# A two-layer diffusion backbone step: later stores, a lead on each load's space, and another table of slots for seven products

## The chip, the core and the metric

The kernel runs on one core of one Trainium2 chip. A core has TensorE (PE, matmuls into eight PSUM banks), VectorE (DVE), ScalarE (ACT), GpSimd (POOL), a queue of transfers issued by SyncE (SP), and sixteen DMA engines. Each engine works off its own instructions in order; they meet through semaphores. The metric is device time of one execution: 3125.22 us is the median of three runs of the kernel before (3124.19 to 3126.09).

## The reference

One inference step over nine row tiles of 128 tokens (T = 0 is the prompt, T = 1 to 8 the sample) with 1024 channels, in float32. Layer 0 mixes tokens with a gated long convolution (Hyena), layer 1 with differential attention, and each is followed by a gated ConvFFN. What the change touches is the ConvFFN:

```python
def conv_ffn(h, w_up, w_dw, b_dw, w_down):      # h (L, 1024), w_up (1024, 5632), w_down (2816, 1024)
    u = dwconv3(h @ w_up, w_dw, b_dw)           # three taps over the tokens
    g, val = jnp.split(u, 2, axis=-1)
    return (jax.nn.silu(g) * val) @ w_down
# around it: hp = rmsnorm(x)*(1+scale)+shift;  x = x + gate * rmsnorm(conv_ffn(hp))
```

The rest (adaLN rows from `SiLU(cond)`, RMSNorms, the Hyena filter and convolution, q/k/v, softmax differences, output projections) is computed as well and is not changed in what it does.

## The kernel before

**Precision.** A float32 product is made of three float32r products: `hi` is a rounded copy (ACT), `lo` the rest (DVE subtracts, or ACT writes `-hi` and a POOL transfer adds the source to it), and PE does hi·hi, hi·lo, lo·hi. `split` (L213) and `halves` (L222) do this; their lines L215, L217, L218 and L220 stand for all splits.

**Column thirds.** Tokens are cut in three groups c = 0, 1, 2 of three tiles, 386 or 388 columns. In `ffn` (L643), for each of 22 blocks j (or g) of 128 channels of the hidden layer, group 0 is done straight: `up` (L659) of the gate and the value weights (24 matmuls each, L667 to L669), `conv`, `gate_val`, and `down0` (18 matmuls into six pinned banks, L690). This is the *up loop*, g = 0 to 21. Groups 1 and 2 are done together: seven products of half-size blocks in the place of eight (a Strassen-like scheme), 12 matmuls each (L746), in the *stage of seven products*: 22 · 7 = 154 slots t, where slot t runs `product(j, q)` with j, q = divmod(t, 7), and then `along(t)`, the other engines' share. The hidden rows go to DRAM (`hid_d`), and the *down stage* reads them back and multiplies by `ffn_down` (L690).

**The table.** `ALONG` (L800) lists for each q what `along` does: `(d, fn, ...)` means fn for block j + d. `load_pair` issues the two weight loads of a block (512 KB each), `total` makes the sums s1 to s4 (DVE, L719), `both` splits with a POOL transfer, `high` (ACT, L729) and `low` (DVE, L732) split without one, `evac` empties banks, `middle`, `side`, `silu`, `finish` do the three-tap filter, the gate and the store. `along` starts at t = -19 (L817), in the last rounds of the up loop: two values of t after each of three places of a round.

**Queues.** SP issues nearly all loads and stores, in program order: one that waits holds up all behind it. Where a load writes into space of an older buffer, it waits until the older one's last reader is done. `postnorm` (L593) is a generator that `advance` steps; `tail(0)` at t = 1 hands three of them to a queue, one step for each block of the seven products, and `tail(1)` does so in the down stage. `extra0` and `extra1` add adaLN rows: loads `adaw`, two DVE passes each (L379).

**Space.** The program is first recorded without a chip (`Dry`). `take` notes for each buffer its size and the count of instructions when it is taken; `note` when it is last used; a last use that is a transfer gets 40 more instructions (`lag`). `place` (L88) then gives addresses, largest buffers first, with as many spare instructions after a buffer's end as fit (up to 1000), trying the whole lag first, then less of it.

Of the kernel before, what the change touches and what calls it, by code (L numbers as in the profile page):

```python
# [15 lines left out]
P = 128  # L16
D = 1024
KT = 8
# [20 lines left out]
class Dry:  # L39
# [14 lines left out]
    def note(self, *args, **kw):  # L54
        for x in (*args, *kw.values()):
            i = self.of.get(x.tensor.name) if isinstance(x, bass.AP) else None
            if i is not None:
                self.lives[i][2:] = self.clock, self.lag
        self.clock += 1

    def transfer(self, *args, **kw):
# [9 lines left out]
    def take(self, shape, dtype, name):  # L71
        t = self.array(shape, dtype)
        size = 4 * math.prod(shape[1:])
        self.of[t.tensor.name] = len(self.lives)
        self.lives.append([-(-size // 32) * 32, self.clock, self.clock, 0])
        return t

    @contextmanager
# [8 lines left out]

def place(lives, room):  # L88

    size, first, until, lag = np.array(lives, dtype=np.int64).T  # L90
    n, end = len(lives), int((until + lag).max()) + 2
    todo = np.lexsort((first, -size))

    def attempt(fill, last):
# [24 lines left out]
        return at.tolist()  # L119

    for part in (4, 3, 2, 1, 0):
        for percent in range(100, 70, -2):
            at = attempt(percent / 100, until + lag * part // 4)
            if at is not None:
                return at
    raise MemoryError("the buffers do not fit")
# [31 lines left out]
def tile_step(tc, nc, a: dict, cst, mem, banks):  # L158
# [38 lines left out]
    def f(ap):  # L197
        return ap.bitcast(F32)
# [392 lines left out]
    def postnorm(T, x, acc, gs, out=None):  # L591
# [49 lines left out]
    SEVEN = ((0, 0), (4, 1), (5, 2), (3, 3), (1, 0), (6, 2), (2, 3))  # L641
    GROUPS = (3, 2, 2, 2, 2, 2, 2, 2, 2, 3)

    def ffn(l, hs, gs, nxt, queue, extra=iter(()), late=(), after=None):

        raw, spl, hid, accs = {}, {}, {}, {}
        ops, rows, sums, out = {}, {}, {}, {}
        hid_d = [tc.dram_tile((P, 6 * P), F32, name=f"hid{l}_{j}") for j in range(NJ)]

        def load(g, parts=range(3)):  # L650
# [51 lines left out]
                    g == 0, g == NJ - 1)  # L702


        def load_pair(j):
            if j < NJ:
                raw[j] = [bt([KT, P], "wr") for _ in range(2)]
                for i in range(2):
                    sync.dma_start(raw[j][i], a["ffn_up"][l, j, :, i])

        lo, hi = slice(0, 4), slice(4, 8)

        def total(i, j):

            a1, a2 = raw[j]
            x, y, op = ((a2[:, lo], a2[:, hi], ALU.add), (sums.get((1, j)), a1[:, lo], ALU.subtract),
                        (a1[:, lo], a2[:, lo], ALU.subtract), (a1[:, hi], sums.get((2, j)), ALU.subtract))[i - 1]
            t = sums[i, j] = bt([4, P], f"s{i}")
            dve.tensor_tensor(out=t, in0=x, in1=y, op=op)  # L719

        def weight(q, j):

            if q in (1, 2, 3, 6):
                return sums[{1: 2, 2: 3, 3: 1, 6: 4}[q], j]
            return raw[j][q == 5][:, lo if q == 0 else hi]

        def high(q, j):
            ops[j, q] = bt([4, P], "hi", F32R), bt([4, P], "lo", F32R)
            act.activation(ops[j, q][0], weight(q, j), AF.Copy)  # L729

        def low(q, j):
            dve.tensor_tensor(out=ops[j, q][1], in0=weight(q, j), in1=f(ops[j, q][0]), op=ALU.subtract)  # L732

        def both(q, j):
            ops[j, q] = halves(weight(q, j), bt, [4, P], True)

        def product(j, q):
            b, d = SEVEN[q]
            if q < 4:
                out[j, d] = ps("pp", True)  # L740
            pt = out[j, d]
            wh, wl = ops.pop((j, q))
            bh, bl = hs["pair"][b]
            for k in range(4):
                for i, (w, t) in enumerate(((wh, bh), (wh, bl), (wl, bh))):
                    pe.matmul(pt[:, 0:NP], w[:, k, :], t[:, k, :], start=q < 4 and k == 0 and i == 0,  # L746
                              stop=k == 3 and i == 2, skip_group_check=q > 3)

        def add(dst, x, pt):
            dve.tensor_tensor(out=dst, in0=pt, in1=x, op=ALU.add)  # L750

        def evac(q, j):
            if q == 0:
                u = sums["u", j] = st([NP], "u")
                act.activation(u, out[j, 0][:, 0:NP], AF.Copy)  # L755
                rows[j] = [st([2 * NP - 2], "row") for _ in range(2)]
            elif q == 1:
                pt, u = out.pop((j, 1)), sums["u", j]
                add(u, u, pt[:, 0:NP])
                unpin(pt)  # L760
            elif q == 2:
                v = sums["v", j] = st([NP], "v")
                add(v, sums["u", j], out[j, 2][:, 0:NP])
            elif q == 3:
                add(rows[j][1][:, NP - 1:], sums.pop(("v", j))[:, 1:], out[j, 3][:, 1:NP])
            elif q == 4:
                pt = out.pop((j, 0))
                act.activation(rows[j][0][:, 0:NP - 1], pt[:, 0:NP - 1], AF.Copy)
                unpin(pt)
            elif q == 5:  # L770
                pt = out.pop((j, 2))
                add(rows[j][1][:, 0:NP - 1], sums["u", j][:, 0:NP - 1], pt[:, 0:NP - 1])
                unpin(pt)
            else:
                pt = out.pop((j, 3))
                add(rows[j][0][:, NP - 1:], sums.pop(("u", j))[:, 1:], pt[:, 1:NP])
                unpin(pt)
# [14 lines left out]
        def side(i, e, j):  # L792
# [4 lines left out]
                rows[j][i] = rows.pop((j, i))  # L797


        ALONG = (  # L800
            ((-1, middle, 1), (0, total, 4), (-2, finish), (-1, evac, 6)),
            ((-1, side, 1, 0), (-1, side, 1, 1), (1, both, 0), (0, high, 6), (0, evac, 0)),
            ((3, load_pair), (-1, middle, 0), (2, total, 1), (0, low, 6), (0, evac, 1)),
            ((1, both, 2), (-1, side, 0, 0), (2, total, 2), (0, evac, 2)),
            ((2, high, 1), (1, both, 3), (-1, side, 0, 1), (0, evac, 3)),
            ((2, low, 1), (1, both, 5), (0, evac, 4)),
            ((-1, silu), (1, both, 4), (2, total, 3), (0, evac, 5)))

        def along(t):
            j, q = divmod(t, 7)  # L810
            for d, fn, *args in ALONG[q]:
                if 0 <= j + d < NJ:
                    fn(*args, j + d)

        def along2(ts):
            for t in (next(ts), next(ts)):
                if t >= -19:  # L817
                    along(t)


# [50 lines left out]
        def main():  # L871
# [25 lines left out]
            advance(queue, -1)  # L897
            for t in range(7 * NJ):
                j, q = divmod(t, 7)
                product(j, q)  # L900
                along(t)
                if t == 1:
                    down0(NJ - 1)
# [13 lines left out]
            for i, (c, m) in enumerate(groups):  # L917
# [1452 lines left out]
```

## Time and profile before

| | |
|---|---|
| median of three runs | 3125.22 us |
| the profiled execution | 3126.71 us, its span 3124.9 us |
| granted clock, mean over the span | 0.992 |
| PE busy, of the span | 97% |
| DVE, ACT, POOL busy | 69%, 55%, 20% |
| DMA queues of SP and of POOL, share of 16 engines | 37.9%, 19.5% |

Matmuls are pipelined: a 386-column one is busy for 0.34 us and the next starts 0.18 us after it, so busy PE is no measure of what could be saved; idle stretches and stretches at the lower clock are.

### The profile page before, as it was taken

How to read it: one execution, taken by the hardware profiler on the slowest of the kernel's cores; microseconds unless marked ns; L12 is line 12 of the kernel's file. 1: busy time of each engine (PE TensorE's matmuls, PEld its weight loads, DVE VectorE, ACT ScalarE, POOL GpSimd, SP SyncE). 2: the span in 40 equal slices, each digit the busy share in tenths (PEclk: the TensorE clock that was granted, in tenths of full speed). 3: DMA queues.
4: the chain of work that ended last, by engine and by line, in shares of the span. 5: the costliest groups of instructions: out<-in, count | busy, mean ns of one | idle time of the engine just before them, and what ended most of it. 6: DMA issues, size and time to landing. Idle time of an engine off the chain costs nothing. (4 is left out here: it accounts for less than half of the span.)

```text
span 3124.9 us, 46695 instructions
## 1 busy us (share of the span) xinstructions
PE 3044.9 (97%) x17332; PEld 2823.7 (90%) x17332; DVE 2143.6 (69%) x3057; ACT 1729.7 (55%) x3185; POOL 619.2 (20%) x1010
## 2 busy tenths in 40 slices
PE   8999999999998999999999999999999999999998
PEld 5999999778888999988899999999888998999987
DVE  5778888756676787776563347789565756777743
ACT  5454445545544777655533348899545546777532
POOL 3111111220001222211143422223220002222100
PEclk9999999999999999999999999999999999999999
DMA  6455546754445898777464464353363246887763
GB/s 254 114 125 119 125 114 157 212 187 141 149 156 154 211 214 209 168 290 258 149 196 148 134 194 110 96 145 106 135 212 140 96 161 153 215 183 182 218 212 119
DMA packets 190136, 520.48 MB, mean 167 GB/s; under 512 B 25730, under 2 KB 53986, under 8 KB 189908
## 3 DMA queue, kind: packets, MB, share of 16 engines
q1 hardware_dynamic: 137428, 394.94, 37.9%
q0 software_dynamic: 52480, 122.56, 19.5%
q8 instruction: 136, 2.23, 0.3%
q14 instruction: 92, 0.75, 0.1%
HBM read 354.50 MB, written 68.13 MB: 135 GB/s over the span
## 5 line engine op out<-in xcount | busy, mean ns | idle before, releaser
L746 PE MATMUL banks<-pair,hi 128*128 128x386 f32 x2464 | 639.1, 341 | 10.0 <-DVE junk L599 9.8
L746 PEld LDWEIGHTS banks<-pair,hi 128*128 128x128 f32 x2464 | 453.2, 190 | 11.4 <-DVE junk L599 10.7
L215 ACT ACTIVATE hi<-wr 128x1024 fp32r<-128x1024 f32 (+1 forms) x400 | 365.2, 913 | 150.4 <-DMA wr<-ffn_up 47.6
L220 DVE TENSOR_TENSOR lo<-wr,hi 128x1024 fp32r<-128x1024 f32 x247 | 305.4, 1237 | 204.8 <-ACT hi L215 203.4
L746 PE MATMUL banks<-pair,lo 128*128 128x386 f32 x1232 | 419.1, 340 | 0.7 <-DMA lo<-wr 0.7
L218 POOL DMA_DIRECT2D lo<-wr x153 | 132.5, 866 | 860.9 <-ACT lo L217 637.4
L690 PE MATMUL banks<-lo,hi 128*128 128x512 f32 x792 | 250.2, 396 | 5.9 <-DVE lo L220 5.9
L690 PE MATMUL banks<-hi,hi 128*128 128x512 f32 x792 | 251.7, 398 | 2.3 <-ACT hi L215 2.3
L690 PE MATMUL banks<-hi,lo 128*128 128x512 f32 x792 | 249.9, 395 | 0.0
L667 PE MATMUL banks<-hi,hi 128*128 128x388 f32 x704 | 240.6, 342 | 8.5 <-ACT hc L510 8.2
L669 PE MATMUL banks<-hi,lo 128*128 128x388 f32 x704 | 239.1, 340 | 1.8 <-DVE lo L220 1.8
L668 PE MATMUL banks<-lo,hi 128*128 128x388 f32 x704 | 239.7, 340 | 0.0
L746 PEld LDWEIGHTS banks<-pair,lo 128*128 128x128 f32 x1232 | 233.3, 189 | 1.0 <-DMA lo<-wr 1.0
L1746 DVE TENSOR_REDUCE mx<-banks 128x1 f32<-128x1152 f32 x128 | 173.4, 1356 | 68.9 <-PE banks L1741 61.7
L1340 PE MATMUL banks<-hi,hi 128*128 128x386 f32 (+1 forms) x576 | 200.4, 348 | 3.8 <-DVE hi L2072 2.5
L1342 PE MATMUL banks<-hi,lo 128*128 128x386 f32 (+1 forms) x576 | 197.1, 342 | 5.8 <-DMA lo<-wr 5.7
L1646 PE MATMUL banks<-hi,hi 128*128 128x384 f32 (+1 forms) x576 | 198.9, 345 | 0.0
L217 ACT ACTIVATE lo<-hi 128x512 fp32r<-128x512 f32 (+1 forms) x265 | 187.0, 706 | 18.6 <-DMA lo<-wr 6.2
L1648 PE MATMUL banks<-hi,lo 128*128 128x384 f32 (+1 forms) x576 | 196.0, 340 | 0.5 <-DVE lo L220 0.5
L1341 PE MATMUL banks<-lo,hi 128*128 128x386 f32 (+1 forms) x576 | 196.3, 341 | 0.0
L1647 PE MATMUL banks<-lo,hi 128*128 128x384 f32 (+1 forms) x576 | 195.9, 340 | 0.0
L690 PEld LDWEIGHTS banks<-lo,hi 128*128 128x128 f32 x792 | 148.8, 189 | 43.2 <-DVE lo L220 9.3
(386 smaller groups left out, 6869.5 us busy)
## 6 DMA issues: line engine op xcount, KB each, us to landing
wr<-ffn_up SPq DMA_DIRECT2D x176, 512.0 KB
wr<-ffn_down SPq DMA_DIRECT2D x132, 512.0 KB
lo<-wr POOLq DMA_DIRECT2D x132, 256.0 KB, 3.9
adaw<-w_adat SPq DMA_DIRECT2D x56, 512.0 KB
lo<-s POOLq DMA_DIRECT2D x88, 256.0 KB, 3.9
x<-x_d SPq DMA_DIRECT2D x33, 512.0 KB
hid<-cv SPq DMA_DIRECT2D x44, 384.0 KB
hd<-hid SPq DMA_DIRECT2D x88, 192.0 KB
```

What stands on the lines that cost most here:

```text
L215: act.activation(hi, src, AF.Copy)
L220: dve.tensor_tensor(out=lo, in0=src, in1=f(hi), op=ALU.subtract)
L667: pe.matmul(pt[:, 0:n], wh[:, k, :], hh[:, k, 0:n], start=k == 0, stop=False)
L668: pe.matmul(pt[:, 0:n], wh[:, k, :], hl[:, k, 0:n], start=False, stop=False)
L669: pe.matmul(pt[:, 0:n], wl[:, k, :], hh[:, k, 0:n], start=False, stop=k == KT - 1)
L690: pe.matmul(accs[c][i][h], s_[:, o:o + P], w_[:, 512 * h:512 * h + 512], start=first and n == 0, stop=last and n == len(parts) - 1)
L746: pe.matmul(pt[:, 0:NP], w[:, k, :], t[:, k, :], start=q < 4 and k == 0 and i == 0, stop=k == 3 and i == 2, skip_group_check=q > 3)
L1340: pe.matmul(pt[:, 0:n], wh[:, k, :], hh[:, k, 0:n], start=k == 0, stop=False)
L1341: pe.matmul(pt[:, 0:n], wh[:, k, :], hl[:, k, 0:n], start=False, stop=False)
L1342: pe.matmul(pt[:, 0:n], wl[:, k, :], hh[:, k, 0:n], start=False, stop=k == KT - 1)
L1646: pe.matmul(pt[:, 0:m], wh[:, k, :], hh[:, k, b:b + m], start=k == 0, stop=False)
L1648: pe.matmul(pt[:, 0:m], wl[:, k, :], hh[:, k, b:b + m], start=False, stop=k == KT - 1)
```

## The change

1. **Lead on loads.** `note` also keeps what the *first* use of a buffer was; if it was a transfer, the buffer gets a lead of 40 recorded instructions, and `place` keeps its space free from that many instructions ahead of where it is taken.
2. **Stores later.** In `postnorm` a step ends between the addition and the store. In the seven products the store of the hidden row, which `finish` issued right behind its multiplication at q = 0, is issued by `store` at q = 3; more slots are run behind the last product for it.
3. **Shorter table.** The seven products become a class `Seven` with its own `ALONG`; the filter's steps stand in `FILL` and come first in a slot. Loads are issued two blocks ahead at q = 0 (before: three blocks at q = 2); s1, s2 and the split of s2 one block ahead (before: two). The first slot run is t = -14 (before: -19).

```diff
-                self.lives[i][2:] = self.clock, self.lag
+                life = self.lives[i]
+                if life[2] is None:
+                    life[4] = self.lag
+                life[2:4] = self.clock, self.lag
...
-        self.lives.append([-(-size // 32) * 32, self.clock, self.clock, 0])
+        self.lives.append([-(-size // 32) * 32, self.clock, None, 0, 0])
...
-            at = attempt(percent / 100, until + lag * part // 4)
+            at = attempt(percent / 100, np.maximum(start - lead * part // 4, 0), until + lag * part // 4)
...
             dve.tensor_tensor(out=x[:, r], in0=x[:, r], in1=junk[:, r], op=ALU.add)
+            if n == 1:
+                yield
             sync.dma_start(dst[:, r], x[:, r])
...
+        FIRST = -14
...
+        def along(self, t):
+            j, q = divmod(t, 7)
+            for d, fn, *args in self.ALONG[q]:
+                if 0 <= j + d < self.steps:
+                    getattr(self, fn)(*args, j + d)
+        def load(self, j):
+            self.raw[j] = self.fetch(j)
+        def spare(self, j):
+            if j in self.whole:                      # whole is empty here
...
         def finish(j):
             cg, cv = rows.pop(j)
             dve.tensor_tensor(out=cv, in0=cg, in1=cv, op=ALU.mult)
-            sync.dma_start(hid_d[j], cv)
+            rows[j] = cv
+        def store(j):
+            sync.dma_start(hid_d[j], rows.pop(j))
...
-            ((3, load_pair), (-1, middle, 0), (2, total, 1), (0, low, 6), (0, evac, 1)),
+            ((1, "total", 1), (0, "low", 6), (0, "evac", 1)),
...
-                if t >= -19:
+                if t >= Seven.FIRST:
...
-                    for n in range(4 * i, 4 * i + 4 - i):
+                    for n in range(4 * i, 4 * i + 4 + 2 * i):
```

What this moves: DVE in the last two rounds of layer 0's up loop, before. The names are tile and number: `s11066` is s1, `s21067` s2 of block 0, `s31079` its s3, `wr` raw weights, `lo1072` the low half for `product(0, 1)`, `adaj`/`adaw` the adaLN rows.

```order
L719 TENSOR_TENSOR s11066_9555<-wr1042_9382 128x512
L719 TENSOR_TENSOR s21067_9558<-s11066_9555,wr1041_9381 128x512
L676 SCALAR_TENSOR_TENSOR cv1068_9585<-banks_65,dw_69,cv1068_9585 128x385
L677 SCALAR_TENSOR_TENSOR cv1068_9585<-banks_65,dw_69,cv1068_9585 128x385
L220 TENSOR_TENSOR lo1070_9593<-wr1059_9506,hi1069_9591 128x1024
L732 TENSOR_TENSOR lo1072_9598<-s21067_9558,hi1071_9597 128x512
L682 TENSOR_TENSOR cv1068_9585<-cv1061_9535,cv1068_9585 128x385
L220 TENSOR_TENSOR lo1074_9605<-cv1068_9585,hi1073_9604 128x385
L379 SCALAR_TENSOR_TENSOR adaj1076_9630,mcol2_98<-adaw1054_9489,cb891_8251 128x1024
L379 SCALAR_TENSOR_TENSOR adaw1054_9489,mcol2_98<-adaw1054_9489,cb892_8252 128x1024
L220 TENSOR_TENSOR lo1078_9637<-wr1045_9389,hi1077_9635 128x1024
L719 TENSOR_TENSOR s31079_9641<-wr1041_9381,wr1042_9382 128x512
```

The same engine and place now, from the last of those rows to the last DVE row ahead of the norm of group 0 (`s31098` is s3 of block 1, `s41101` s4 of block 0).

```order
L680 TENSOR_TENSOR s11079_9660<-wr1057_9492 128x512
L774 SCALAR_TENSOR_TENSOR cv1080_9687<-banks_65,dw_69,cv1080_9687 128x385
L775 SCALAR_TENSOR_TENSOR cv1080_9687<-banks_65,dw_69,cv1080_9687 128x385
L680 TENSOR_TENSOR s21083_9699<-s11079_9660,wr1056_9490 128x512
L780 TENSOR_TENSOR cv1080_9687<-cv1076_9648,cv1080_9687 128x385
L223 TENSOR_TENSOR lo1089_9715<-cv1080_9687,hi1088_9714 128x385
L382 SCALAR_TENSOR_TENSOR adaj1091_9741,mcol2_98<-adaw1069_9602,cb891_8239 128x1024
L382 SCALAR_TENSOR_TENSOR adaw1069_9602,mcol2_98<-adaw1069_9602,cb892_8240 128x1024
L223 TENSOR_TENSOR lo1093_9745<-wr1060_9500,hi1092_9744 128x1024
L694 TENSOR_TENSOR lo1085_9703<-s21083_9699,hi1084_9701 128x512
L680 TENSOR_TENSOR s31098_9763<-wr1074_9619,wr1075_9621 128x512
L680 TENSOR_TENSOR s41101_9784<-wr1056_9490,s21083_9699 128x512
```

Block 0's s1, s2 and the low half of s2 have moved from the last round but one to the last round, to where block 1's stood; the low half for `product(0, 1)` is now two DVE rows from the end.

SP at the start of the seven products, before (`x` a row tile's load and store by `postnorm`, `hid<-cv` a hidden row's store).

```order
L588 DMA x1139_9970<-x_d0_72 128x1024
L709 DMA wr1154_10084<-ffn_up 128x1024
L709 DMA wr1155_10086<-ffn_up 128x1024
L609 DMA x_d0_72<-x1139_9970 128x1024
L782 DMA hid0_0_6176<-cv1145_10030 128x768
L709 DMA wr1180_10265<-ffn_up 128x1024
L709 DMA wr1181_10267<-ffn_up 128x1024
L588 DMA x1192_10331<-x_d1_73 128x1024
L782 DMA hid0_1_6177<-cv1171_10211 128x768
```

SP at the same place now.

```order
L591 DMA x1133_9947<-x_d0_72 128x1024
L806 DMA wr1140_10010<-ffn_up 128x1024
L806 DMA wr1141_10011<-ffn_up 128x1024
L806 DMA wr1166_10191<-ffn_up 128x1024
L806 DMA wr1167_10193<-ffn_up 128x1024
L822 DMA hid0_0_6173<-cv1139_10006 128x768
L614 DMA x_d0_72<-x1133_9947 128x1024
L806 DMA wr1192_10370<-ffn_up 128x1024
L806 DMA wr1193_10372<-ffn_up 128x1024
L822 DMA hid0_1_6174<-cv1165_10186 128x768
```

Each store has moved behind the next pair of loads, and a row tile's store behind one pair more. PE's order is the same but for four groups of transposes in layer 0's second down group (a row tile's norm steps come one step later each).

## Rows read from the trace of the kernel before

**Rows 1.** Busy time by stretch; last columns: granted clock, DMA share, GB/s.
```profile
690.00:1008.00 318.00, 296.54 (x1518) 272.41 (x1516) 216.03 (x289) 152.42 (x236) 12.97 (x19) 0.97 0.45 152
1008.00:1334.00 326.00, 325.80 (x1826) 325.43 (x1827) 253.33 (x376) 226.85 (x364) 90.81 (x107) 0.99 0.85 203
2311.00:2610.00 299.00, 289.20 (x1518) 269.35 (x1516) 191.07 (x245) 151.25 (x235) 13.21 (x19) 0.99 0.42 141
```
**Rows 2.** Waits of SP's queue, 690 to 1008 us: total, times, longest.
```profile
SPq L654 <- DVE lo L220: 43.8, 10, 7.4
...
SPq L414 <- ACT xn L455: 10.2, 1, 10.2
```
**Rows 3.** Timeline, 785 to 803 us: start, duration, idle before and its releaser.
```profile
787.08 0.33 SPq L414 DMA_DIRECT2D G<-m_d  x1
...
794.18 1.06 ACT L215 ACTIVATE hi<-wr 128x1024 fp32r<-128x1024 f32 x1 [7.42 <-DMA wr<-ffn_up]
...
797.83 1.09 PE L507 MATMUL banks<-ident,xn 128*128 128x128 f32 x4 [2.93 <-DVE cv L677]
...
801.29 0.69 PE L667 MATMUL banks<-hi,hi 128*128 128x388 f32 x1 [2.38 <-ACT hc L510]
```
**Rows 4.** Stretches at the lower clock, columns as in Rows 1.
```profile
384.50:391.30 6.80, 5.97 (x18) 5.98 (x19) 6.66 (x9) 0.00 (x0) 0.00 (x0) 0.50 0.05 18
565.40:575.60 10.20, 7.63 (x18) 4.83 (x17) 10.03 (x19) 10.01 (x12) 4.13 (x5) 0.50 1.07 224
797.50:804.30 6.80, 4.10 (x13) 3.73 (x14) 3.12 (x6) 4.26 (x10) 0.00 (x0) 0.50 0.20 78
998.90:1002.30 3.40, 3.40 (x10) 2.64 (x9) 0.88 (x2) 1.02 (x2) 1.31 (x2) 0.50 0.73 126
```
**Rows 5.** PE's waits, 870 to 1000 us.
```profile
PE banks L690 <- DVE lo L220: 5.2, 4, 2.2
PE banks L690 <- ACT hi L215: 2.3, 2, 1.5
```
**Rows 6.** Timeline, 370 to 386 us.
```profile
375.52 0.82 SPq L1328 DMA_DIRECT2D wr<-hy_in  x2
...
375.62 0.90 POOL L218 DMA_DIRECT2D lo<-wr  x1 [6.21 <-ACT lo L217]
...
385.32 0.69 PE L1342 MATMUL banks<-hi,lo 128*128 128x388 f32 x1 [2.98 <-DMA lo<-wr]
```
**Rows 7.** PE's waits, 60 to 558 us.
```profile
PE banks L1342 <- DMA lo<-wr: 5.7, 5, 3.0
```
**Rows 8.** DMA issues: queue, count, KB each, median us to landing.
```profile
lo<-wr POOLq DMA_DIRECT2D x21, 512.0 KB, 4.8
```
**Rows 9.** PE's waits, 560 to 640 us.
```profile
PE banks L1953 <- DMA w<-wo: 2.6, 1, 2.6
PE banks L1953 <- DMA w<-wor: 2.1, 1, 2.1
```
**Rows 10.** The chain of waits, 2601 to 2640 us: start, us, what.
```profile
2601.55 3.64 DMA lo<-wr
...
2605.26 0.63 ACT lo L217
...
2606.79 0.58 ACT junk L595 x2
...
2609.84 30.17 PE banks L746 x160
```
**Rows 11.** Timeline of PE and DVE, 2596 to 2610 us.
```profile
2598.36 0.34 PE L746 MATMUL banks<-pair,lo 128*128 128x386 f32 x1
...
2600.06 0.69 DVE L732 TENSOR_TENSOR lo<-s,hi 128x512 fp32r<-128x512 f32 x1
...
2609.84 0.69 PE L746 MATMUL banks<-pair,hi 128*128 128x386 f32 x1 [5.38 <-DVE junk L599]
```
**Rows 12.** Longest wait of SP's queue, 1008 to 1334 us.
```profile
SPq L782 <- DVE cv L781: 191.6, 20, 16.8
```

More of the change, by code (lines that the diff above doesn't have):

```diff
@@ L88, in place, with attempt @@
 def place(lives, room):
-    size, first, until, lag = np.array(lives, dtype=np.int64).T
+    size, start, until, lag, lead = np.array(lives, dtype=np.int64).T
     n, end = len(lives), int((until + lag).max()) + 2
-    todo = np.lexsort((first, -size))
-    def attempt(fill, last):
+    todo = np.lexsort((start, -size))
+    def attempt(fill, first, last):
         spare = np.full(n, -1)
@@ L638, in __init__, with total, weight, high @@
             self.ahead, self.main, self.step = ahead, main, ahead.step
-    SEVEN = ((0, 0), (4, 1), (5, 2), (3, 3), (1, 0), (6, 2), (2, 3))
+    class Seven:
+        TAKE = ((0, 0), (4, 1), (5, 2), (3, 3), (1, 0), (6, 2), (2, 3))
+        ALONG = (
+            ((2, "load"), (0, "total", 4), (0, "spare"), (-1, "evac", 6)),
+            ((1, "both", 0), (0, "high", 6), (0, "evac", 0)),
+            ((1, "total", 1), (0, "low", 6), (0, "evac", 1)),
+            ((1, "both", 2), (1, "total", 2), (0, "evac", 2)),
+            ((1, "high", 1), (1, "both", 3), (0, "evac", 3)),
+            ((1, "low", 1), (1, "both", 5), (0, "evac", 4)),
+            ((1, "both", 4), (2, "total", 3), (0, "evac", 5)))
+        FIRST = -14
+        def __init__(self, steps, n, fetch, hs, block, whole=()):
+            self.steps, self.n, self.fetch, self.hs, self.block, self.whole = steps, n, fetch, hs, block, whole
+            self.raw, self.ops, self.sums, self.out = {}, {}, {}, {}
+        def along(self, t):
[5 more added lines that the diff above has]
+            self.raw[j] = self.fetch(j)
+        def total(self, i, j):
+            (a11, a12), (a21, a22) = ((w[:, 0:4], w[:, 4:8]) for w in self.raw[j])
+            x, y, op = ((a21, a22, ALU.add), (self.sums.get((1, j)), a11, ALU.subtract),
+                        (a11, a21, ALU.subtract), (a12, self.sums.get((2, j)), ALU.subtract))[i - 1]
+            t = self.sums[i, j] = bt([4, P], f"s{i}")
+            dve.tensor_tensor(out=t, in0=x, in1=y, op=op)
+        def weight(self, q, j):
+            if q in (1, 2, 3, 6):
+                return self.sums[{1: 2, 2: 3, 3: 1, 6: 4}[q], j]
+            return self.raw[j][q == 5][:, slice(0, 4) if q == 0 else slice(4, 8)]
+        def high(self, q, j):
+            self.ops[j, q] = bt([4, P], "hi", F32R), bt([4, P], "lo", F32R)
+            act.activation(self.ops[j, q][0], self.weight(q, j), AF.Copy)
+        def low(self, q, j):
+            hi, lo = self.ops[j, q]
+            dve.tensor_tensor(out=lo, in0=self.weight(q, j), in1=f(hi), op=ALU.subtract)
+        def both(self, q, j):
+            self.ops[j, q] = halves(self.weight(q, j), bt, [4, P], True)
+        def spare(self, j):
+            if j in self.whole:
+                self.ops[j, 7] = halves(self.raw[j][1][:, 0:4], bt, [4, P], True)
+        def product(self, j, q):
+            b, d = self.TAKE[q]
+            if q < 4:
+                self.out[j, d] = ps("pp", True)
+            pt = self.out[j, d]
+            wh, wl = self.ops[j, q] if j in self.whole else self.ops.pop((j, q))
+            bh, bl = self.hs["pair"][b]
+            for k in range(4):
+                for i, (w, t) in enumerate(((wh, bh), (wh, bl), (wl, bh))):
+                    pe.matmul(pt[:, 0:self.n], w[:, k, :], t[:, k, :], start=q < 4 and k == 0 and i == 0,
+                              stop=k == 3 and i == 2, skip_group_check=q > 3)
+        def evac(self, q, j):
+            n = self.n
+            if q == 0:
+                u = self.sums["u", j] = st([n], "u")
+                act.activation(u, self.out[j, 0][:, 0:n], AF.Copy)
+                return
+            if q == 2:
+                v = self.sums["v", j] = st([n], "v")
+                dve.tensor_tensor(out=v, in0=self.out[j, 2][:, 0:n], in1=self.sums["u", j], op=ALU.add)
+                return
+            pt = self.out[j, 3] if q == 3 else self.out.pop((j, self.TAKE[q][1]))
+            if q == 1:
+                u = self.sums["u", j]
+                dve.tensor_tensor(out=u, in0=pt[:, 0:n], in1=u, op=ALU.add)
+            elif q == 4:
+                dst, cols = self.block(j, 0, 0)
+                act.activation(dst, pt[:, cols], AF.Copy)
+            else:
+                dst, cols = self.block(j, *{3: (1, 1), 5: (1, 0), 6: (0, 1)}[q])
+                x = self.sums.pop(("v", j)) if q == 3 else self.sums["u", j]
+                dve.tensor_tensor(out=dst, in0=pt[:, cols], in1=x[:, cols], op=ALU.add)
+            if q != 3:
+                unpin(pt)
@@ L646, in ffn @@
         raw, spl, hid, accs = {}, {}, {}, {}
-        ops, rows, sums, out = {}, {}, {}, {}
+        rows = {}
         hid_d = [tc.dram_tile((P, 6 * P), F32, name=f"hid{l}_{j}") for j in range(NJ)]
@@ L702, in down0 @@
                     g == 0, g == NJ - 1)
[L705 to L755, printed above, removed]
-                rows[j] = [st([2 * NP - 2], "row") for _ in range(2)]
[L757 to L777, printed above, removed]
@@ L779, in finish, with load_two, block @@
+        def load_two(j):
+            ws = [bt([KT, P], "wr") for _ in range(2)]
+            for i in range(2):
+                sync.dma_start(ws[i], a["ffn_up"][l, j, :, i])
+            return ws
+        def block(j, r, c):
+            if j not in rows:
+                rows[j] = [st([2 * NP - 2], "row") for _ in range(2)]
+            return rows[j][r][:, (NP - 1) * c:(NP - 1) * (c + 1)], slice(c, NP - 1 + c)
+        seven = Seven(NJ, NP, load_two, hs, block)
         def finish(j):
@@ L797, in side @@
                 rows[j][i] = rows.pop((j, i))
-        ALONG = (
-            ((-1, middle, 1), (0, total, 4), (-2, finish), (-1, evac, 6)),
-            ((-1, side, 1, 0), (-1, side, 1, 1), (1, both, 0), (0, high, 6), (0, evac, 0)),
-            ((3, load_pair), (-1, middle, 0), (2, total, 1), (0, low, 6), (0, evac, 1)),
[L804 to L807, printed above, removed]
+        FILL = (((-1, middle, 1), (-2, finish)), ((-1, side, 1, 0), (-1, side, 1, 1)), ((-1, middle, 0),), ((-1, side, 0, 0), (-2, store)),
+                ((-1, side, 0, 1),), (), ((-1, silu),))
         def along(t):
             j, q = divmod(t, 7)
-            for d, fn, *args in ALONG[q]:
+            for d, fn, *args in FILL[q]:
                 if 0 <= j + d < NJ:
                     fn(*args, j + d)
+            seven.along(t)
         def along2(ts):
             for t in (next(ts), next(ts)):
-                if t >= -19:
+                if t >= Seven.FIRST:
                     along(t)
@@ L899, in main @@
                 j, q = divmod(t, 7)
-                product(j, q)
+                seven.product(j, q)
                 along(t)
```

## The prediction

> **What bounds the kernel now.** I read the busy time by stretch first [rows 1]. In the stage of seven products of layer 0 (1008 to 1334 us) PE is busy for 325.80 of 326.00 us at a granted clock of 0.99: TensorE is the bound there, and nothing that only moves stores, loads or the other engines' share can shorten it by more than a few tenths. The longest wait of SP's queue lies in that very stage: 191.6 us in 20 waits, longest 16.8, for the hidden rows that it is to store [rows 12]. The reader is to see that these 191.6 us cost PE nothing. They are where the change looks largest, and not where it can gain.
>
> The stretch worth reading is the up loop, where PE has gaps. Layer 0's (690 to 1008) and layer 1's (2311 to 2610) hold the same 1518 matmuls, and take 318.00 and 299.00 us [rows 1], 19.0 apart. PE is idle for 318.00 − 296.54 = 21.5 us of the one and 299.00 − 289.20 = 9.8 of the other: 11.7 of the 19.0 are idle, the other 7.3 slower matmuls. SP's waits come next [rows 2]. Its loads of weights (L654) wait ten times, 43.8 us in all, until DVE has read the older buffer in their space, and one load that is not a weight (L414, the row of gates G) waits 10.2 us for the tile xn that held its space, with all weight loads queued behind it. The timeline [rows 3] then shows what that does to PE, and the stretches at the lower clock [rows 4] what follows each gap: TensorE's clock is granted at 0.50, that is 1.2 GHz in place of 2.4, and half of PE's busy time there is lost.
>
> So what can be gained is a list of places where a load came late.
>
> **The change part by part.** *The lead.* Its gain is the sum of those places.
>
> (a) 794 us. G is issued at 787.08, 10.2 us late, the weights behind it after it. ACT's split of one of them starts at 794.18, after 7.42 us idle; PE then waits 2.93 us at 797.83 and 2.38 at 801.29 [rows 2, 3]. From 797.5 to 804.3 the clock is 0.50 and PE is busy for 4.10 us [rows 4], of which 2.05 would go at full clock. Together 2.93 + 2.38 + 2.05 = 7.4 us. With the space of each load free 40 recorded instructions ahead, the G load no longer waits where it is queued. I take all of it; the other end is nothing, if ACT has something else late there.
>
> (b) 870 to 1000 us. `down0` waits 5.2 us for low halves of DVE and 2.3 for high ones of ACT [rows 5]. Two stretches of 3.40 us at clock 0.50, of which one stands in [rows 4], cost 3.40 / 2 = 1.7 each. 7.5 + 3.4 = 10.9 us. These splits are of weights and of hidden rows in turn; only the part behind a late load goes. I take half, 5.5; the ends are 0 and 10.9.
>
> (c) 382 us, Hyena. Two loads of raw weights and a POOL transfer into a low half are released within 0.1 us of each other (375.52 and 375.62). It ends PE's wait of 2.98 us at 385.32, so it took 9.7 us at most [rows 6]; the median of 21 such transfers is 4.8 us [rows 8]. The clock then is 0.50 for 5.97 us of busy PE [rows 4], so 3.0 more: 6.0 together. With the lead the two loads go out earlier than the transfer. I take 4 (the ends: 6.0, and 0 if they meet another transfer). The other four of these waits sum to 5.7 − 3.0 = 2.7 us [rows 7]; I take 1.
>
> (d) 565 us, output projection. PE waits 2.6 and 2.1 us for transfers of `wo` and `wor` [rows 9], and 7.63 us of PE run at half clock [rows 4], 3.8 lost: 8.5. But ACT is busy there for 10.01 of 10.20 us and DVE for 10.03 [rows 4]: with earlier loads their own work would be late next. I take 1.5 (ends 0 and 8.5).
>
> (e) 2609.84 us. PE waits 5.38 us for a bank of the norm [rows 11]. The chain [rows 10] tells why: a transfer into a low half lands at 2605.19, ACT's negated half `lo` starts only at 2605.26 since it overwrites the raw weights which that transfer reads, and the squares (L595) come behind it, at 2606.79. In the new plan of addresses that `lo` lies on a buffer that DVE has read by about 2598.6, so ACT is freed before the transfer ends. What the transfer can hold ACT for is at most its own 3.64 us; I take two thirds, 2.4, since the squares also need the last group's products. The ends are 0 and 3.64. In layer 0 the same `lo` still lies behind such a transfer: nothing there.
>
> *The shorter table.* s1, s2 and the low half of s2 of block 0 move one round later, to two DVE rows from the end of the up loop. PE reads that low half for `product(0, 1)` at 2598.36; the DVE row that now stands there ended at 2600.06 + 0.69 = 2600.75 [rows 11], so PE would wait 2.4 us. This falls ahead of the wait of 5.38, which DVE and ACT end and not PE: the products that are delayed only fill it. I cost it at 0; if (e) shrinks to under 2.4, up to 2.4 a layer shows, so 4.8 is its upper end. Within the stage a DVE row may come 7 slots later than before, but each still leaves its product two or more slots, and a slot is twelve matmuls at 0.18 us, 2.1 us. PE's cover there is whole [rows 1], and I take 0.
>
> *Stores later.* The hidden row's store goes behind the next pair of loads, so these no longer queue behind the 191.6 us [rows 12]. PE is not waiting for them: 0. What the store adds is two tiles held three slots longer. The store of a row tile, a step later, moves four groups of transposes in the second down group of layer 0 by one place; 0, for PE's work there is the same.
>
> *New meetings.* Loads that go out earlier ride beside other transfers. Between 0 and the 5.8 each that the second rival has below, I take 2 us in all.
>
> **Sum.** 7.4 + 5.5 + 4 + 1 + 1.5 + 2.4 − 2 = 19.8 us, from the profiled execution's 3126.7 to 3106.9. That execution was 1.5 us above the median of 3125.22, so the forecast for the median is 3105.4, say 3105.5. In the likeliest case it lies between 3125.2 − 7.4 = 3118, where only (a) goes, and 3125.2 − (7.4 + 10.9 + 6.0 + 2.7 + 1.5 + 2.4) = 3094, where all of (b) and (c) go and no transfers meet.
>
> **Rivals.** Faster or slower is told from no change by 0.2%, 6.25 us. *1. The up loop is set by DVE and ACT, not by loads.* For it: the largest waits in [rows 5] name DVE and ACT, not a load, and in layer 1, where SP serves the same weights, PE is still idle for 9.8 us. Against it: the 7.42 us in [rows 3] end on a load. Then half of (a) goes, and what the lead frees elsewhere is late by another engine: 3125.2 − 3.7 = 3121.5, inside that bound. Chance 0.14.
>
> *2. Slower: the early loads take the DMA engines from POOL's transfers.* Its place is Hyena, where each group of weights has a transfer into its low half, 21 of them [rows 8], and PE uses that half soon after. The row at 375.62 is the price: beside two loads a transfer took up to 9.7 us in place of 4.8. The time from issue to PE's need there was 385.32 − 2.98 − 375.62 = 6.7 us, so a transfer that meets two loads is up to 3.0 us late, and the half clock after it costs another 3.0 [rows 4, 6]: say 5.8 each. Before, four more of the 21 were late, by 0.7 us each [rows 7]; if the earlier loads now meet five transfers more, 5 × 5.8 = 29 us come in, against gains of 7.4 + 5.5 + 1.5 + 2.4 = 16.8: 3125.2 + 12.2 = 3137. It makes the kernel slower from the third meeting (17.4 against 16.8). Against it: a load that is free to go is spread over the time that the queue leaves it, and the two met because one instruction released both. Chance 0.08. The Trainium skill speaks for this rival: its page "DMA: Bandwidth & Descriptors", section "Queues, rings and completion order", says that each DMA engine takes turns between the queues that have work for it, a packet at a time, so a queue with loads in it halves what another gets. By that rule 4.8 us would become 9.6, and the 9.7 of the row agrees.
>
> *3. The change doesn't do what it says.* The planner may give up part of the lead to make all fit. The new plan keeps the whole lead, and the order of SP and DVE stands as described: no chance of its own.
>
> **How the numbers follow.** 0.78 for the forecast, 0.14 for rival 1, 0.08 for rival 2. The forecast's own range, 3094 to 3118, is faster than the bound throughout (under 3119). The range of 8 in 10 reaches from 3094 to 3122, which takes in rival 1's time. Chances: faster 0.78, same 0.14, slower 0.08.
>
> **What would show it.** (a) right: no PE wait of over 1 us and no clock of 0.50 between 785 and 805 us, the G load issued with the loads around it; SP's L654 waits well below 43.8 us. Layer 0's up loop then takes 318 − 7.4 − 5.5 = 305 us, and its idle falls to about 11. (b) right: the waits of L690 at half of 7.5. (c) right: no wait of 2.98 near 382. (e) right: the wait ahead of the seven products near 3 us in layer 1. Both stages of seven products should stay at 326 and 325 us. The short table shows as a wait of PE of about 2.4 us for `lo` L694 at the end of the up loop. Wrong would be: an up loop of layer 0 at 315 or more with waits that name DVE or ACT (rival 1), or transfers into low halves of 9 us and more at four or more places (rival 2).

## The result and the profile after

The changed kernel takes 3102.15 us, median of four runs (3101.47 to 3102.43), beside 3124.7 for the kernel before in the same comparison: ratio 0.9929 (95% interval 0.9912 to 0.9946), 22.5 us less. The forecast was 3105.5. The profiled span is 3100.2 us against 3124.9.

Counting PE's matmuls from the first gives the same places in both traces. Busy time by stretch, columns as in [rows 1]: layer 0's up loop, its seven products, layer 1's up loop.

```profile
690.20:991.70 301.50, 291.69 (x1517) 270.21 (x1515) 213.77 (x286) 150.84 (x232) 12.35 (x18) 0.99 0.48 162
991.70:1315.20 323.50, 323.46 (x1827) 323.11 (x1828) 257.24 (x381) 228.95 (x367) 91.19 (x108) 1.00 0.85 205
2290.40:2589.00 298.60, 291.01 (x1518) 270.61 (x1518) 189.78 (x242) 150.13 (x234) 13.07 (x19) 0.99 0.42 140
```

Two thirds of the 24.7 us between the two spans lie in the first row: 301.5 in place of 318.0, PE idle for 9.8 us in place of 21.5, as much as it was in layer 1 before (there it is 7.6 now). The timeline there, 765 to 800 us (answers to [rows 3]):

```profile
770.86 0.80 SPq L417 DMA_DIRECT2D G<-m_d  x2
771.72 1.10 SPq L752 DMA_DIRECT2D wr<-ffn_up  x2
...
783.81 1.06 ACT L218 ACTIVATE hi<-wr 128x1024 fp32r<-128x1024 f32 x1
```

and the stretch in which PE waited and the clock was 0.50 (answers to the third of [rows 4]):

```profile
785.00:805.00 20.00, 19.41 (x107) 18.27 (x106) 10.58 (x14) 9.63 (x18) 2.13 (x1) 1.00 0.30 106
```

G goes out 16 us earlier than at 787.08, the weights right behind it, and neither the waits of 2.93 and 2.38 us nor the low clock are left. PE's longest waits, 690 to 990 us (answers to [rows 5]):

```profile
PE banks L713 <- DVE lo L694: 4.3, 1, 4.3
PE banks L765 <- ACT hc L513: 3.2, 5, 0.8
PE banks L788 <- DVE lo L223: 1.2, 3, 0.5
```

`down0` (L788) now waits 1.2 us for low halves, not 5.2, and a new wait of 4.3 us stands on top: the low half for `product(0, 1)`. Right behind it PE waits for a bank of the norm, in layer 0 too. That wait in the kernel before, and the stretch at the lower clock that began in it and reached 4.5 us into the seven products:

```profile
PE banks L746 <- DVE junk L599: 4.5, 1, 4.5
```

```profile
1005.70:1012.50 6.80, 4.47 (x14) 4.47 (x15) 5.28 (x9) 3.90 (x12) 3.52 (x7) 0.50 0.40 71
```

and the wait in the changed one (both waits from 870 to 1012 us):

```profile
PE banks L713 <- DVE junk L602: 1.1, 1, 1.1
```

The seven products of layer 0 now run at a clock of 1.00 throughout and are 2.6 us shorter. The other 5 to 6 us are spread over later stages: 1.5 in layer 1's seven products, under 2 in each other.

SP's weight loads wait no less than before (43.8 us in [rows 2]):

```profile
SPq L752 <- DVE lo L223: 48.9, 13, 7.1
```

The queue's total says nothing on lateness: SP now stands at a load earlier, and waits there. What does is ACT's wait for those loads. The same stage of the kernel before, and of the changed one:

```profile
ACT hi L215 <- DMA wr<-ffn_up: 35.6, 11, 7.4
```

```profile
ACT hi L218 <- DMA wr<-ffn_up: 2.2, 2, 1.8
```

PE's waits in Hyena (60 to 558 us): one of the kernel before that [rows 7] leaves out, then those of the changed kernel, and at the output projection (556 to 640; [rows 9]):

```profile
PE banks L324 <- DMA lo<-adar: 2.1, 2, 1.4
```

```profile
PE banks L327 <- DMA lo<-adar: 7.2, 5, 3.5
...
PE banks L1377 <- DMA lo<-wr: 1.0, 2, 0.7
```

```profile
PE banks L1988 <- DMA w<-wo: 4.3, 3, 2.7
...
PE banks L1988 <- DVE y L223: 1.2, 1, 1.2
PE banks L1988 <- DMA w<-wor: 0.8, 1, 0.8
```

The wait of 2.98 at 382 is gone; one of 3.5 us for an adaLN half (`adar`) has come. PE's waits for POOL's transfers in Hyena sum to 8.2 us in place of 7.8: they moved from the weights to the adaLN halves. At the output projection nothing is won: 4.3 + 0.8 for 2.6 + 2.1.

### The profile page after: what moved, and what is told of

Its sections match the earlier page's. It is cut to its first block, busy times and chain, and to the rows that moved or that the text cites. A ratio compares the mean times of both kernels' runs of the same rounds, so it can differ in the third digit from the quotient of the medians.

```text
span 3100.2 us, 46634 instructions
## 1 busy us (share of the span) xinstructions
PE 3035.9 (98%) x17332; PEld 2819.8 (91%) x17332; DVE 2142.9 (69%) x3057; ACT 1727.2 (56%) x3185; POOL 623.0 (20%) x1010
## 3 DMA queue, kind: packets, MB, share of 16 engines
q0 software_dynamic: 52480, 122.56, 19.8%
## 4 chain that ended last, share of the span: by engine, by line
PE 65%; DVE 2%; ACT 2%; issue 2%; POOL 1%; DMA 0%; POOLq 0%; SPq 0%; DVEq 0%; ACTq 0%
PE banks L713 21%; PE banks L788 15%; PE banks L1776 4%; PE banks L1807 4%; PE banks L1682 3%; PE banks L1683 3%; PE banks L1681 3%; PE banks L765 3%; PE banks L767 3%; PE banks L766 3%; PE banks L1988 2%; PE banks L1797 2%; DVE lo L223 0%; ACT obuf L1824 0%; ACT hc L513 0%
## 5 line engine op out<-in xcount | busy, mean ns | idle before, releaser
L788 PE MATMUL banks<-hi,hi 128*128 128x512 f32 x792 | 250.3, 396 | 0.1
L788 PE MATMUL banks<-lo,hi 128*128 128x512 f32 x792 | 248.4, 394 | 1.9 <-DVE lo L223 1.9
L788 PE MATMUL banks<-hi,lo 128*128 128x512 f32 x792 | 247.7, 393 | 0.0
L788 PEld LDWEIGHTS banks<-lo,hi 128*128 128x128 f32 x792 | 148.4, 188 | 37.8 <-DVE lo L223 4.3
```

Source lines behind the costliest of these rows:

```text
L788: pe.matmul(accs[c][i][h], s_[:, o:o + P], w_[:, 512 * h:512 * h + 512], start=first and n == 0, stop=last and n == len(parts) - 1)
```

## The experiments

The prediction lets the lead bring the gain. The rivals here: the shorter table brings it, since fewer buffers are alive (theory B, later R), or any new plan of addresses moves the late loads by chance (C). Each kernel was timed beside the kernel before, whose medians in these comparisons were 3124.6 to 3126.7 us. Lengths of stages, in us, are those of one trace each, between the same matmuls as the first row's 60, 558, 690, 1008 and 1334 (2311 and 2610 for layer 1). "Level" is the share of the room up to which `place` hands out spare instructions behind a buffer's end: it tries 100, 98, 96, ... and takes the first at which all buffers find an address (worked out from the planner's code, as is the share of the lead).

| kernel | table | lead | level | us | ratio to before, 95% | Hyena | up loop 0 | seven 0 | up loop 1 |
|---|---|---|---|---|---|---|---|---|---|
| before | old | none | 94 | 3124.7 | 1 | 498.1 | 318.0 | 326.1 | 299.2 |
| changed | short | whole | 94 | 3102.2 | 0.9912 to 0.9946 | 496.6 | 301.5 | 323.5 | 298.6 |
| lead_alone | old | 3/4 | 96 | 3148.3 | 1.0061 to 1.0089 | 526.4 | 301.7 | 331.3 | 300.9 |
| lead_out | short | none | 98 | 3097.5 | 0.9901 to 0.9928 | 488.0 | 302.1 | 323.5 | 298.4 |
| stores_alone | old | none | 94 | 3128.9 | 1.0001 to 1.0019 | 495.8 | 318.6 | 329.4 | 299.3 |
| table_alone | short | none | 98 | 3097.6 | 0.9898 to 0.9925 | 488.9 | 302.0 | 323.4 | 298.7 |
| ballast | short | none | 98 | 3110.7 | 0.9944 to 0.9968 | 488.6 | 309.9 | 326.4 | 299.1 |
| fill_94 | short | none | 94 | 3118.9 | 0.9973 to 0.9991 | 493.2 | 317.0 | 325.4 | 298.9 |
| low_early | short | none | 98 | 3091.2 | 0.9877 to 0.9904 | 488.4 | 297.8 | 323.4 | 296.1 |
| lead_late | old | 3/4, not in Hyena | 96 | 3117.3 | 0.9964 to 0.9985 | 490.1 | 302.5 | 330.2 | 301.1 |
| before_97 | old | none | 97 | 3118.2 | 0.9965 to 0.9984 | 489.4 | 309.6 | 332.1 | 299.6 |
| table_95 | short | none | 95 | 3115.2 | 0.9947 to 0.9975 | 493.5 | 313.7 | 324.0 | 298.7 |
| after_95 | short | whole | 95 | 3103.3 | 0.9913 to 0.9938 | 501.8 | 300.7 | 323.3 | 296.7 |
| gates_lead | short | G alone | 94 | 3112.2 | 0.9944 to 0.9971 | 493.3 | 309.4 | 325.6 | 296.7 |

**One part at a time.** lead_alone is the kernel before with part 1 alone; lead_out takes only the lead out of the changed kernel:

```diff
-            at = attempt(percent / 100, np.maximum(start - lead * part // 4, 0), until + lag * part // 4)
+            at = attempt(percent / 100, start, until + lag * part // 4)
```

> The kernel before with part 1 alone: the lead. Its planner fits with three quarters of the lead and of the lag after a transfer (30 instructions each). Theory A, the lead brings the gain by earlier loads in the up loop of layer 0: 3106 to 3113 us, against 3124.7 before; no clock of 0.50 near 797 us, layer 0's up loop 12 to 17 us shorter, ACT's waits for raw weights there under 10 us in place of 35.6. Theory B, the shorter table brings it (a block fewer in flight, so space is free by itself): 3119 to 3126 us. Theory C, any new plan of addresses moves the late loads by chance: anywhere between 3105 and 3130, and the same for each kernel with another plan.

> The changed kernel with the lead taken out of the planner, all else as it is. Theory A: 3116 to 3127 us, ACT's waits for raw weights in layer 0's up loop back above 25 us in total. Theory B: 3100 to 3107 us, as the changed kernel's 3102.2. Theory C: anywhere in 3105 to 3130.

Both times of theory A failed: alone the lead makes the kernel 0.75% slower, and without it the changed kernel loses nothing (3097.5). No theory foresaw 3148.3. Yet lead_alone has the short up loop, 301.7 us, as the prediction said it would; what it gives back is Hyena, 526.4 in place of 498.1, and 5 us in the seven products. The trace shows how, in Hyena. DVE writes an intermediate tile there, fTW. Its waits before that write, in the kernel before and in lead_alone (60 to 550 us); then ACT's and PE's waits in lead_alone (60 to 590 us):

```profile
DVE fTW L951 <- PE banks L324: 4.9, 6, 0.8
```

```profile
DVE fTW L954 <- DMA lo<-adar: 18.3, 3, 7.4
DVE fTW L954 <- ACT cb L1359: 17.9, 3, 6.8
```

```profile
ACT hi L218 <- DVE fTW L954: 22.5, 7, 4.2
```

```profile
PE banks L1345 <- DMA lo<-wr: 17.8, 7, 3.3
```

In lead_alone DVE waits 36.2 us before it writes fTW, for a transfer and for a row of ACT's whose results it does not read: the space is still in use. ACT's split of an adaLN half waits for DVE, and the split of the weights comes later in ACT's order; so POOL's transfer goes out later, and PE waits for the low half seven times, in place of the 5.7 us of [rows 7]. At five of these seven waits the clock falls to 0.50, for 3.4 us each. The transfers themselves are hardly slower, a median of 5.1 us against 4.8 [rows 8]:

```profile
lo<-wr POOLq DMA_DIRECT2D x21, 512.0 KB, 5.1
```

The seven that PE waits for took 6.9 to 8.0 us; in the kernel before, PE waited under 0.7 us for three that took 6.9 to 7.2, and 1.0 and 3.0 us for two of 10.0 and 9.7. So room is the currency: space kept free ahead of loads is taken from tiles that engines write, which have no lead.

stores_alone has part 2 on the kernel before; table_alone has part 3 and neither of the others:

```diff
-            if n == 1:
-                yield
...
-            rows[j] = cv
+            sync.dma_start(hid_d[j], cv)
...
-        ... ((-1, side, 0, 0), (-2, store)), ...
+        ... ((-1, side, 0, 0),), ...
```

> The kernel before with part 2 alone: hidden rows stored at q = 3, row tiles a step later. Theories A and B: 3122 to 3127 us, no change, since SP's long waits for hidden rows lie in a stage where PE is never idle. A theory that these stores held up the loads that PE lacks: 3108 to 3116 us. Theory C: 3105 to 3130, as this too has another plan of addresses.

> The changed kernel without the lead and without the later stores, so the shorter table alone. Theory A: 3121 to 3130 us; the wait for the low half of product (0, 1) at the end of each up loop shows, 4 us in layer 0 and 2 us in layer 1. Theory B: 3102 to 3110 us. Theory C: 3105 to 3130.

The stores bring nothing: +4 us on the old table, at the edge of what can be told, and lead_out, which has them, equals table_alone to 0.2 us. The table alone brings the whole gain and a little more, 27 us. This is theory B, whose ranges lead_out and table_alone still miss by 2.5 and 4.4 us on the fast side. C is not what is seen for gains of this size: kernels with different plans that share table and level (stores_alone and before; lead_out and table_alone) agree within some 4 us, stage for stage. A few us in one stage may still come with a plan alone (Hyena in after_95, the seven products in before_97).

**What of the table it is.** ballast holds 16 KB idle per partition where the old table held its third block:

```diff
+                if g == NJ - 4:
+                    ballast = [bt([KT, P], "ballast") for _ in range(4)]
...
+                if t == 7 * (NJ - 2):
+                    for x in ballast:
+                        pool.memset(x[:, 0, 0:1], 0.0)
```

> The kernel of table_alone (3097.6 us) with four idle buffers of 4 KB per partition held from the last four rounds of each up loop to two blocks before the end of the seven products, so that the tightest place needs 96% of the room, as in the kernel before, and not 90%; two times four tiny POOL memsets end them, under 1 us. Theory R (room: the shorter table has fewer buffers alive, so the planner has more slack and fewer writes wait for a reader): 3106 to 3125 us, and waits of ACT for raw weights in layer 0's up loop back above 15 us. Theory O (order: it is the order of the other engines' work that changed): 3096 to 3100 us.

fill_94 forces the level on table_alone (`range(94, 70, -2)` for `range(100, 70, -2)`), table_95 does so with `range(95, 70, -1)`, and before_97 is the kernel before with `range(100, 70, -1)`.

> The kernel of table_alone with the planner told to start at 94% of the room when it hands out spare time, which is where the kernel before ended, and not at 98%. If the level of spare time over the whole program is what frees Hyena (6.5 us at 300 to 400 us of the kernel before): 3101 to 3108. If the shorter table acts by its own place alone: 3096 to 3100.

> The kernel of table_alone with the planner held to 95%: between fill_94 (3118.9) and table_alone at 98% (3097.6). Theory L, if spare time falls off evenly with the level: 3110 to 3118. If it is one threshold, at which some few buffers lose their spare time: near 3119 or near 3098, and the trace has all of the late loads near 795 and 889 us, or none.

> The kernel before, with one number changed: the planner steps down by 1% and not by 2% when it looks for a level at which all buffers fit, so it ends at 97% of the room and not at 94%. Table, stores and the order of all instructions are the old ones. Theory L (the level of spare time decides, and the shorter table only lets the planner find a higher one): 3098 to 3112 us, without the waits of 2.9 and 2.4 us near 795. Theory R (the table's own 12 KB decide): 3118 to 3127.

The ballast costs 13 us with the order unchanged: theory R, not O, though ACT's waits for raw weights came to 14.0 us, not above 15. Most of its loss, 7.9 us, is in the up loop; there two waits in the last round are new, 3.5 us at the bank and 2.6 for a transfer into a low half, while that for DVE's low half, 4.2 in table_alone, is a little shorter (690 to 992 us):

```profile
PE banks L711 <- DVE junk L602: 3.5, 1, 3.5
...
PE banks L711 <- DVE lo L692: 3.0, 1, 3.0
...
PE banks L711 <- DMA lo<-wr: 2.6, 1, 2.6
```

The level costs more than the ballast: with the short table at 94 the time is 3118.9, beyond both ranges, and the up loop is 317.0 us long, like the old one. The trace of fill_94 has the waits of [rows 3] back, almost to the number:

```profile
790.46 1.06 ACT L218 ACTIVATE hi<-wr 128x1024 fp32r<-128x1024 f32 x1 [7.37 <-DMA wr<-ffn_up]
...
794.11 0.63 PE L510 MATMUL banks<-ident,xn 128*128 128x128 f32 x4 [2.87 <-DVE cv L773]
...
797.57 0.69 PE L763 MATMUL banks<-hi,hi 128*128 128x388 f32 x1 [2.83 <-ACT hc L513]
```

So at one level, 94, the lead is worth 3118.9 − 3102.2 = 16.7 us (the two also differ by the stores, worth nothing), 15.5 of them in that up loop. It is no gain over leaving it out, since without it the short table fits at 98, where the same loads are early enough. The level by itself is only part of the account: before_97 gains 8 us, at the edge of theory R, where L expected 12 to 27; it keeps the waits near 790 (3.65 and 2.83 us) and loses 6 us in the seven products. table_95, at 3115.2, is within the range of an even fall, but has both of those waits (3.38 and 2.37 us), as one threshold would have it: it settles nothing between the two. What the table gives is room, used twice: at its own place, and through the level of 98, at which the old table's buffers do not fit (98 and 96 fail, 97 fits). At 94 the short table is still 6 us faster than the kernel before; no run parts its room from its order there.

**The finer step on the changed kernel.**

> The changed kernel with the same finer steps: the whole lead at 95% and not at 94%. Theory L: a little faster than 3102.2, 3096 to 3101 us, the gain in Hyena and the output projection (500 to 560 us). If the lead has freed the loads whatever the level: 3101 to 3104.

No gain (3098.18 to 3107.06 in five runs), against theory L: one more per cent does nothing where the lead already frees the loads. Hyena is 5 us longer.

**Where the lead hurts.** lead_late is lead_alone with one line more:

```diff
+    lead = np.where(start < 5000, 0, lead)
```

> The kernel of lead_alone (3148.3 us) with the lead only for buffers taken from layer 0's ConvFFN on (recorded instruction 5000), none in Hyena. If Hyena's 28 us of loss there come from the lead of Hyena's own loads, which takes the spare time from the tiles that ACT writes: 3108 to 3122 us. If they come from the plan as a whole (three quarters of the lag after transfers): 3140 to 3150.

31 us come back, the Hyena stage is 490.1 us long in place of 526.4, and PE's waits there fall from 17.8 us in seven to

```profile
PE banks L1346 <- DMA lo<-wr: 1.9, 4, 0.9
```

The lead in Hyena was the whole loss there, and DVE's waits before fTW are gone from its list. It was DVE's tile that lost the space, not ACT's as the expectation has it. The up loop keeps its 302.5. Of the 15.5 us won there and the 8 in Hyena the kernel as a whole keeps 8: the seven products, the output projection and later stages are longer.

**The load of G alone.** gates_lead gives fill_94 a lead for eight buffers, the G rows:

```diff
-                    life[4] = self.lag
+                    life[4] = self.lag if i in self.early else 0     # early: tiles named G
```

> The kernel of fill_94 (3118.9 us) with a lead of 40 instructions for eight buffers alone, the rows of gates G, again at 94% of the room. If the wait of the load of G for the tile xn is what made the weights late near 790 us: that load goes out at about 770 us in place of 783, PE's waits of 3.0 and 3.0 us there and the stretch at clock 0.50 go, 3109 to 3114 us. If the load of wp ahead of it in the queue (which waits 21 us there) sets the time: the waits stay, 3117 to 3121 us.

SP's timeline in fill_94, and in gates_lead:

```profile
769.19 0.33 SPq L413 DMA_DIRECT2D wp<-norm_w  x1
769.62 14.12 SPq L417 DMA_DIRECT2D G<-m_d  x2
```

```profile
769.04 0.33 SPq L415 DMA_DIRECT2D wp<-norm_w  x1
769.47 0.99 SPq L419 DMA_DIRECT2D G<-m_d  x2
770.51 1.16 SPq L752 DMA_DIRECT2D wr<-ffn_up  x2
```

Both loads of G go within a microsecond, the weights 13 us earlier, the two waits of PE are gone, the clock from 780 to 800 us is 1.00, and the kernel is 6.7 us faster. In layer 0's up loop it is 7.6 us (317.0 to 309.4): one wait of one small load, and what was queued behind it, was worth about what the prediction had put on it, 7.4.

**The low half.** In low_early, on table_alone, the low half for product 1 stands a slot earlier:

```diff
-            ((1, "high", 1), (1, "both", 3), (0, "evac", 3)),
-            ((1, "low", 1), (1, "both", 5), (0, "evac", 4)),
+            ((1, "high", 1), (1, "both", 3), (0, "evac", 3), (1, "low", 1)),
+            ((1, "both", 5), (0, "evac", 4)),
```

> The kernel of table_alone with the low half for product (0, 1) and its successors one slot earlier (q = 4, behind the bank's emptying). The waits for it at the end of the up loops (4.3 us in layer 0, 2.4 in layer 1) go. If these delay the norm behind them and so the end: 3089 to 3094 us. If the norm's bank wait only grows by as much: 3096 to 3099.

3091.2 us, the fastest of all, 11 under the changed kernel; 6.4 under table_alone at the same level. PE's waits around the first products, in table_alone and then in low_early:

```profile
973.35 0.69 PE L711 MATMUL banks<-pair,lo 128*128 128x386 f32 x1 [4.18 <-DVE lo L692]
...
982.24 0.62 PE L711 MATMUL banks<-pair,hi 128*128 128x386 f32 x2 [0.17 <-DVE junk L602]
```

```profile
975.05 0.73 PE L786 MATMUL banks<-lo,hi 128*128 128x512 f32 x2 [1.35 <-DVE lo L223]
...
980.29 0.63 PE L711 MATMUL banks<-pair,hi 128*128 128x386 f32 x2 [1.29 <-DVE junk L602]
```

4.18 + 0.17 became 1.35 + 1.29 in layer 0. The up loops (which end at the bank wait) are 4.2 and 2.6 us shorter, more than the waits alone. The rest is the clock, which fell to 0.50 during the stall in table_alone and stayed at 1.00 in low_early:

```profile
972.10:978.90 6.80, 5.55 (x16) 5.07 (x17) 2.40 (x4) 1.92 (x4) 1.70 (x2) 0.50 0.71 121
```

```profile
966.00:984.00 18.00, 15.35 (x76) 13.31 (x75) 12.44 (x20) 13.56 (x30) 7.79 (x12) 1.00 0.90 220
```

Half of the 5.55 us of PE's work in the first row is 2.8 us lost.

## Why the prediction was right, and where its reasons were not

The direction, the size and the stage were right, and (a) as well: layer 0's up loop was to fall from 318 to 305 and fell to 301.5; the waits of [rows 3] and [rows 5] went as described. gates_lead gives 6.7 us for (a), taken at 7.4. One sign of (a) failed: SP's waits for weights did not fall well below 43.8 us, they came to 48.9. (b) came nearly whole, not by half; the new stall of 4.3 us took part of it back.

That the sum of 19.8 came so near the 22.5 measured (24.7 between the profiled executions) is in part luck. The up loop gave 3.6 us more than its 12.9. Hyena and the output projection gave 0.3 together (1.5 won, 1.2 lost) in place of 6.5, and layer 1's up loop 0.6 in place of 2.4. The seven products, said to stay at 326 and 325, gave 2.6 and 1.5: PE is busy throughout there, but at half clock where the stretch at 0.50 that began in the bank wait ran into the stage, and that place is not in the sum.

What failed is the step "*The lead.* Its gain is the sum of those places". That sum counts the waits which a lead removes, and forgets what it is paid with; the shorter table, which carried the gain, stands in it at 0. The prediction laid all that the new plan frees to the lead; the short table's plan does the same without it. The lead is worth −16.7 us on the short table at level 94, and +23.7 on the old one, where the planner had to come down to three quarters of lead and lag. From the kernel before to the changed one, the table is what makes the lead affordable, and a table without the lead does as well or better (3097.6; the two ratio intervals overlap, so the 4.6 us between them are likely and not shown).

(c) The wait at 382 went, but in Hyena as a whole 1.5 us were won, not 5; a wait for an adaLN half (3.5 us, with a granted clock of 0.83 over the 10 us from it on) took part of the rest. table_alone and lead_out run Hyena in 488 to 489 us, 8 less; at the changed kernel's own level fill_94 takes 493.2, so the lead costs 3.4 there and the level the rest. Whether the 8.2 us of waits are the new meetings that were put at 2 us is not shown. (d) Nothing came of the 1.5. (e) The bank wait of 5.38 in layer 1 fell more than expected, and the reason given held: ACT's `lo` no longer waits for the transfer (2.64 us before its 2605.26). But the squares (L598) now wait for PE. The timeline after, 2575 to 2590 us (answers to [rows 11]):

```profile
2580.23 0.68 DVE L694 TENSOR_TENSOR lo<-s,hi 128x512 fp32r<-128x512 f32 x1
...
2580.97 0.69 PE L713 MATMUL banks<-pair,lo 128*128 128x386 f32 x1 [2.24 <-DVE lo L694]
...
2581.97 0.63 ACT L220 ACTIVATE lo<-hi 128x512 fp32r<-128x512 f32 x1
...
2585.55 0.60 ACT L598 ACTIVATE junk<-banks 128x512 f32<-128x512 f32 x1 [2.06 <-PE banks L788]
...
2588.71 0.62 PE L713 MATMUL banks<-pair,hi 128*128 128x386 f32 x2 [0.18 <-DVE junk L602]
```

5.38 became 2.24 + 0.18: the gap moved ahead, and with it the stretch at the lower clock, 3.4 us from 2580.6 on, into the stage, which is only 0.6 us shorter. The prediction put the late low half at 0, as it would only fill the bank wait, and allowed up to 2.4 us a layer if (e) shrank that wait. The size of the stall was right for layer 1 (2.4 us, measured 2.24; 4.3 in layer 0), its cover was not: `down0` of the last block, whose sums the norm squares, stands behind `product(0, 1)` on PE, so a stall there delays the norm too. low_early puts it, with the lower clock that came with it, at 6.4 us for both layers, above the 4.8 of its upper end. Layer 0, where the prediction expected nothing of (e), had the same bank wait (4.5 us, now 1.1).

Rival 1 is out: ACT's waits for raw weights went with the gain. Rival 2 prices a meeting at 5.8 us where its own terms, 3.0 and 3.0, give 6.0; nothing hangs on it. It is not what the changed kernel did, but for lead_alone it had the right place and nearly the right price (seven waits of up to 3.3 us, +28 us in Hyena) and the wrong mechanism: the transfer's median went to 5.1 us, and the seven took 8.0 at most, not the 9.7 of [rows 6]; they were issued late. The Trainium skill ("DMA: Bandwidth & Descriptors", "Queues, rings and completion order") says that each DMA engine takes turns between the queues with work for it; the doubling was the prediction's estimate from that. Single transfers came near it (9.7 and 10.0 us in the kernel before, 9.1 in the changed one); as the cause of lead_alone's loss these runs do not show it.

## What to carry to other kernels

Room is shared: before a load gets space ahead of time, ask which other tile loses it, and test the rule alone. When several edits land together, undo each: here one of three carried the gain, another carried it only at a worse plan, and their sum was no better than the one alone. A stall is covered by a later wait only if what that wait waits for does not itself stand behind the stall.

## What was not expected of the hardware

A queue's total waiting is no sign of late data: SP's weight loads waited 43.8 us before and 48.9 after, while ACT's waits for what they bring fell from 35.6 to 2.2. And one small load, G, held for 13 us at the head of the queue, costs 6.7 us of the kernel, through PE waits of 2.87 and 2.83 us in fill_94 and the granted clock of 0.50 that set in behind the first of them, from 796.1 to 802.8 us.
